# Two transformer blocks on one core: chosen rows fetched into the weights' ring and worked off in pairs from within the query projection on

## The chip, the cores and the metric

The kernel runs on one core of one Trainium2 chip. A time is the device time of one execution in microseconds (us), and what counts is the median of several runs. TensorE is called PE, VectorE DVE, ScalarE ACT, GpSimd POOL and SyncE SP, as the profile does.

## What is computed

A sequence of 256 tokens with 1024 numbers each goes through two blocks. The first has a gated mixer, a recurrent mixer and 32 experts, the second two attentions and a layer that looks up rows (`peer`). The change lies in that last layer and in the final norm behind it:

```python
def peer(xn, w_q, sub_keys, u, v):                      # xn: 256 tokens x 1024
    q = (xt @ w_q).reshape(t, PEER_HEADS, 2, PEER_HALF)  # 8 heads, two halves of 128
    sc = jnp.einsum("thpc,hpnc->thpn", q, sub_keys)      # 128 scores for each half
    top_s, top_i = lax.top_k(sc, PEER_TOPK)              # the best 16 of each half
    cand_s = top_s[:, :, 0, :, None] + top_s[:, :, 1, None, :]
    cand_i = top_i[:, :, 0, :, None] * PEER_NKEYS + top_i[:, :, 1, None, :]
    best_s, best_pos = lax.top_k(cand_s, PEER_TOPK)      # 16 of the 256 sums
    idx = jnp.take_along_axis(cand_i, best_pos, axis=-1) # 8 x 16 = 128 rows of 16384
    gate = jax.nn.softmax(best_s, axis=-1)
    ...
        act = jnp.einsum("cd,ced->ce", xc, u[ic])
        hid = jax.nn.gelu(act) * gc
        return jnp.einsum("ce,ced->cd", hid, v[ic])
x = x + peer(rmsnorm(x, norm2_g), ...); return rmsnorm(x, norm_f_g)
```

Each token picks 128 rows of a table whose rows hold 1024 numbers of u and 1024 of v, in fp32. For 256 tokens this is 32768 rows of 8 KB, 268.4 MB in all.

## The kernel before, in words

Everything is in one program whose order is written by hand (`manual_schedule`): each engine takes its instructions in the order in which the Python code emits them. Weights come over SP's queue in tiles of 16 KB per partition (4096 fp32 numbers) through a ring of `NRING` = 6 buffers, `rg[0]`; `get` and `free` move it on. A weight tile is used in eight slices; `chunk` splits a slice into a high and a low part, `sh` on ACT (line 164) and `sl` on DVE (line 165), up to two slices ahead of PE. `drive` runs a projection slice by slice and takes `per` steps of a second piece of work between slices.

The last layer handles the 256 tokens as two halves `tt` of 128, a token on each partition. After `rows_rstd` and `row_scale` come `WARM[5]` = 20 idle multiplications, the transposes of `to_T` and four query projections `projT` (line 234), each over one tile of `w_q` and two heads. `best` (lines 1204 to 1231) multiplies the queries with the keys (line 1210) and finds the best 16 of each half on DVE, for both `tt`. `choose(tt, i)` (lines 1136 to 1189) makes 32 row numbers `ei` and gates `gt` for one `tt` and two heads out of it, in 11 steps. `choose(0, 0)` rides in the third projection. The other seven are spread over the row loop, a step behind each row.

"Row k" below is one fetch of the loop `for k in range(256)`: the k-th chosen row of all 128 tokens of a half, 128 x 8 KB = 1 MB, by one indirect DMA from POOL (line 1259). `fetch` has `NR` = 13 buffers of its own, `rw`, on the right side of the memory where the ring was, and goes out `AHEAD` = 9 rows early. `first` (line 1264) multiplies the u half with the normed token `xr` on DVE and sums. `gelu` runs on ACT for four rows at a time, `second` multiplies with the gates on DVE (line 1274), makes a diagonal `dg` for each row on ACT (line 1277) and adds the v half to `acc` on PE (line 1280). `acc`, four banks of PSUM, is started with the residual by four multiplications (line 1245) just ahead of the loop. `final(0)` is emitted at row 132, `final(1)` at the end.

The lines that set the pace of the loop:

```python
for k in range(256):
    while nk < min(256, k + AHEAD):
        ...
        fetch(nk)
    first(k)
    if k % 4 == 3: gelu(k // 4)
    if k % 4 == 1 and k > 4: second(k // 4 - 1)
```

## Time and profile before

| | |
|---|---|
| median of 3 runs | 1532.22 us (1531.4 to 1534.25) |
| the profiled execution's own time | 1527.95 us |
| its span, first to last instruction | 1526.2 us |
| granted TensorE clock, mean of the span | 0.955 |
| PE / DVE / ACT / POOL busy | 86% / 52% / 26% / 27% |
| read from HBM in the span | 528.08 MB, 347 GB/s |
| of it chosen rows (POOL's queue) | 268.45 MB |

All times in rows are microseconds from the start of the span. The granted clock is a share of 2.4 GHz: 1.00 is 2.4 and 0.50 is 1.2 GHz. A PE multiplication of fp32 stands as two records in the trace, so a row of the loop has four records on PE.

### The profile page before, as it was taken

What the parts mean: (1) busy time and instruction counts of PE and PEld (TensorE: products, weight loads), DVE (VectorE), ACT (ScalarE), POOL (GpSimd) and SP (SyncE); (2) the same over time, 40 slices, a digit from 0 to 9 for tenths busy, and PEclk for the clock granted to TensorE, in tenths of its full rate; (3) what the DMA queues carried; (4) which work ended last, traced back from release to release, by engine and by line L of the source; (5) the groups of instructions that cost most, each with busy time, mean ns of one, the idle gap of its engine ahead of it and who ended that gap; (6) DMA issues with size and microseconds to landing.
All of it is one profiled execution on the core that took longest, in us unless ns stands there. A gap on an engine that the chain in (4) does not pass through costs nothing.

```text
span 1526.2 us, 16072 instructions
## 1 busy us (share of the span) xinstructions
PE 1307.3 (86%) x5543; PEld 708.8 (46%) x5543; DVE 794.6 (52%) x1852; ACT 395.1 (26%) x881; POOL 406.5 (27%) x363
## 2 busy tenths in 40 slices
PE   9899999999999898999999577878877778778776
PEld 7676344434434433978979433333332323333332
DVE  4766222222222223677677998778554545544443
ACT  6634011110111112556655232222111111111111
POOL 1211000000000002142120354444444445445441
PEclk9999999999999999999999889899999999999998
DMA  9526899999999999553220869999999999999993
GB/s 390 220 111 275 363 428 427 427 427 426 428 427 427 427 429 426 211 207 125 111 97 1 350 275 419 421 419 420 420 420 419 420 420 420 419 420 420 420 420 163
DMA packets 57747, 530.21 MB, mean 347 GB/s; under 512 B 6592, under 2 KB 6848, under 8 KB 9408
## 3 DMA queue, kind: packets, MB, share of 16 engines
q0 software_dynamic: 37936, 272.65, 43.4%
q1 hardware_dynamic: 19440, 256.35, 40.4%
q8 instruction: 46, 0.75, 0.2%
q14 instruction: 37, 0.30, 0.1%
q10 hardware_dynamic: 288, 0.16, 0.0%
HBM read 528.08 MB, written 1.05 MB: 347 GB/s over the span
## 4 chain that ended last, share of the span: by engine, by line
DMA 33%; PE 23%; issue 8%; DVE 6%; POOL 5%; ACT 1%; POOLq 0%; DVEq 0%; ACTq 0%
DMA rw<-in_uv_dram,ei 27%; PE b L234 6%; PE b L816 5%; POOL rw L1259 4%; DMA w<-in_w_gate_dram 4%; PE acc L1280 2%; PE b L854 2%; DMA w<-in_w_down_dram 2%; PE b L263 1%; DVE jk L1264 1%; PE b L247 1%; DVE sl L165 1%; PE b L763 1%; PE b L777 1%; PE b L111 1%
## 5 line engine op out<-in xcount | busy, mean ns | idle before, releaser
L1280 PE MATMUL acc<-rw,dg 128*128 128x512 f32 x1024 | 498.3, 644 | 151.6 <-ACT dg L1277 151.6
L1264 DVE SCALAR_TENSOR_TENSOR jk<-rw,xr 128x1024 f32<-128x1024 f32 x256 | 314.2, 1227 | 245.0 <-DMA rw<-in_uv_dram,ei 243.8
L1280 PEld LDWEIGHTS acc<-rw,dg 128*128 128x128 f32 x1024 | 205.2, 206 | 444.7 <-issue 230.5
L1259 POOL DMA_INDIRECT rw<-in_uv_dram,ei x256 | 306.5, 1197 | 385.6 <-PE acc L1280 283.6
L816 PE MATMUL b<-w,xg 128*64 128x512 f32 x1024 | 238.5, 605 | 10.5 <-DMA w<-in_w_gate_dram 8.2
L165 DVE TENSOR_TENSOR sl<-w,sh 128x512 fp32r<-128x512 f32 (+1 forms) x193 | 137.4, 719 | 81.4 <-ACT sh L164 80.6
L1277 ACT ACTIVATE dg<-kc,act 128x128 f32<-128x128 f32 x256 | 81.8, 390 | 284.3 <-DVE act L1274 284.3
L816 PEld LDWEIGHTS b<-w,xg 128*64 128x64 f32 x1024 | 82.5, 139 | 155.0 <-issue 134.0
L164 ACT ACTIVATE sh<-w 128x512 fp32r<-128x512 f32 (+1 forms) x200 | 120.7, 620 | 106.9 <-PE b L234 63.4
L854 PE MATMUL b<-w,hT 128*64 128x512 f32 x512 | 116.2, 595 | 6.6 <-ACT hT L125 5.5
L810 POOL TENSOR_TENSOR Dw<-Dw,Wt 128x256 f32<-128x256 f32 x16 | 9.9, 618 | 389.7 <-DVE Dw L809 389.7
L234 PE MATMUL b<-nT,sh 128*128 128x256 f32 x576 | 106.8, 286 | 3.3 <-ACT sh L164 1.7
L234 PEld LDWEIGHTS b<-nT,sh 128*128 128x128 f32 x576 | 89.0, 190 | 9.4 <-issue 4.7
L779 DVE TENSOR_TENSOR res<-res,b 128x512 f32<-128x512 f32 x64 | 40.0, 683 | 100.9 <-PE b L777 100.9
L234 PE MATMUL b<-nT,sl 128*128 128x256 f32 x288 | 81.8, 284 | 3.0 <-DVE sl L165 2.9
L859 DVE SCALAR_TENSOR_TENSOR eo<-b,gs,eo 128x512 fp32r<-128x512 f32 x32 | 24.0, 751 | 114.7 <-ACT eo L858 112.0
L854 PEld LDWEIGHTS b<-w,hT 128*64 128x64 f32 x512 | 39.0, 137 | 71.4 <-issue 61.0
L1269 ACT ACTIVATE act<-act 128x4 f32<-128x4 f32 x64 | 13.1, 205 | 227.1 <-DVE jk L1264 227.1
L823 DVE TENSOR_TENSOR hs<-hs,b 128x512 f32<-128x512 f32 x16 | 11.0, 688 | 105.9 <-PE b L816 105.9
L247 PE MATMUL b<-sh,nT 128*128 128x512 f32 (+1 forms) x192 | 58.2, 380 | 0.5 <-ACT sh L164 0.5
L234 PEld LDWEIGHTS b<-nT,sl 128*128 128x128 f32 x288 | 54.7, 190 | 4.1 <-DVE sl L165 4.1
L858 ACT ACTIVATE eo<-b,gs 128x512 fp32r<-128x512 f32 x32 | 22.0, 687 | 115.5 <-PE b L854 89.0
(407 smaller groups left out, 1323.5 us busy)
## 6 DMA issues: line engine op xcount, KB each, us to landing
w<-in_w_gate_dram SPq DMA_DIRECT2D x32, 2048.0 KB, 18.4
w<-in_w_up_dram SPq DMA_DIRECT2D x32, 2048.0 KB, 20.5
w<-in_w_down_dram SPq DMA_DIRECT2D x32, 2048.0 KB, 18.3
w<-in_w_in_dram SPq DMA_DIRECT2D x13, 2048.0 KB, 16.6
w<-in_w_out_dram SPq DMA_DIRECT2D x4, 2048.0 KB, 13.2
w<-in_w_q_dram SPq DMA_DIRECT2D x4, 2048.0 KB, 8.1
rw<-in_uv_dram,ei POOLq DMA_INDIRECT x256, 15.7
w<-in_w_in_dram SPq DMA_DIRECT2D x4, 512.0 KB, 7.3
```

The source lines that it names most:

```text
L164: nc.scalar.activation(hi, src, AF.Copy)
L165: (eng or nc.vector).tensor_tensor(lo, src, hi.bitcast(F32), op=ALU.subtract)
L234: nc.tensor.matmul(dst, l[:, c * 128:(c + 1) * 128], x[:, r, k, :], start=(k == 0 and c % 2 == 0 and i == 0), stop=(k == nk - 1 and i == 2 ...
L247: nc.tensor.matmul(bs[tt][:, :n], x[:, l, k, tt * 128:(tt + 1) * 128], r[:, :n], start=(k == 0 and i == 0), stop=(k == 7 and i == 2))
L779: nc.vector.tensor_tensor(rs, rs, b, op=ALU.add)
L816: nc.tensor.matmul(dst[64 * j:64 * j + 64, :], xg[:, k, 2 * pr + j, :], w[j][:, k * 512:(k + 1) * 512], start=(k == 0), stop=(k == 7))
L854: nc.tensor.matmul(bh[half][64 * j:64 * j + 64, :], hT[:, f, 64 * j:64 * j + 64], w[j][:, f * 1024 + half * 512:f * 1024 + half * 512 + 51 ...
L859: nc.vector.scalar_tensor_tensor(eo[:, 1, v], bh[half], wc, eo[:, 0, v].bitcast(F32), op0=ALU.mult, op1=ALU.subtract)
L1259: nc.gpsimd.indirect_dma_start(got[k], None, A["uv"], bass.IndirectOffsetOnAxis(ap=ei[tt][:, s:s + 1], axis=0))
L1264: nc.vector.scalar_tensor_tensor(junk, got[k][:, 0:D], 1.0, xr[:, tt], op0=ALU.mult, op1=ALU.mult, accum_out=act[tt][:, s:s + 1])
L1277: nc.scalar.activation(dg, ident, AF.Copy, scale=v[:, j:j + 1])
L1280: nc.tensor.matmul(acc[tt][hf], dg, rw[:, D + hf * 512:D + (hf + 1) * 512], start=False, stop=(s + j == 127), skip_group_check=True)
```

## The change

Rows no longer have buffers of their own. `fetch` takes a tile of the weights' ring, which holds two rows, and fetches a pair of rows into it. A pair goes out when its row numbers are there (`chosen`) and when the tiles of weights and of rows that are not yet freed leave one of the six buffers. The ring stays open to the end; `NR` and `AHEAD` are gone.

The choices stand in a list `todo`, those of half 0 first, each `seq(best(tt, i), choose(tt, i))` with 3 + 11 steps for one half alone. The scores `sc` of all heads get a place of their own; the keys are multiplied right behind each projection. A projection but the last takes `RQ` = 1.6 steps of `todo` per slice (`filler`), and `fetch` is tried behind each step. With the fourth projection the rows are worked off beside it: `alongside` emits a pair (`places`) and two steps of `todo` per slice, and goes on so to the end. A pair is two `first`, one `gelu` over two rows, and for each row the gate as a copy with a scale on ACT (line 1269 of the changed kernel), the diagonal and the two multiplications. The last pair is worked off row by row. The start of `acc` moves ahead of the norm. `norm_f` is loaded behind the four projections.

```diff
-        with pool("p4", 1) as p4, pool("p4b", 2) as p4b:
+        def fetch():
+            while row_st["next"] < min(256, chosen[0]) and len(src) + row_st["next"] // 2 < st["freed"] + row_st["done"] // 2 + NRING:
+                k = row_st["next"]
+                w = rg[0].tile([128, 4096], F32, tag="w", name="w")
+                for j in range(2):
+                    tt, s = divmod(k + j, 128)
+                    got[k + j] = rw = w[:, j * 2 * D:(j + 1) * 2 * D]
+                    nc.gpsimd.indirect_dma_start(rw, None, A["uv"], bass.IndirectOffsetOnAxis(ap=ei[tt][:, s:s + 1], axis=0))
+                row_st["next"] += 2
+        def step():
+            while todo and next(todo[0], StopIteration) is StopIteration:
+                todo.pop(0)
+            fetch()
+        for tt in range(2):
+            for hf in range(2):
+                nc.tensor.matmul(acc[tt][hf], ident, res[:, tt, hf * 512:(hf + 1) * 512], start=True, stop=False, skip_group_check=True)
...
-        pr_ = pk.enter_context(pool("pr", NR, side="right"))
...
+        def second(k, n):
+            tt, s = divmod(k, 128)
+            v = act[tt][:, s:s + n]
             nc.scalar.activation(v, v, AF.Gelu)
-            nc.vector.tensor_tensor(v, v, gt[tt].rearrange("p h r -> p (h r)")[:, s:s + 4], op=ALU.mult)
-            for j in range(4):
+            for j in range(n):
+                nc.scalar.activation(v[:, j:j + 1], v[:, j:j + 1], AF.Copy, scale=gf[tt][:, s + j:s + j + 1])
                 dg = pd.tile([128, 128], F32, name="dg")
                 nc.scalar.activation(dg, ident, AF.Copy, scale=v[:, j:j + 1])
...
+        def places():
+            for k in range(0, 256, 2):
+                while row_st["next"] <= k + 1:
+                    step()
+                n = 1 if k == 254 else 2
+                for j in range(0, 2, n):
+                    for i in range(j, j + n):
+                        first(k + i)
+                    second(k + j, n)
+                fetch()
+                if k == 132:
+                    final(0)
+                yield
+        def alongside():
+            for _ in pl:
+                step()
+                yield
+                step()
+        for i in range(4):
+            qT = pq2.tile([128, 4, T], F32, name="qT")
+            drive(projT(8, n4, lambda hh, b: evac(flat(qT[:, 2 * hh:2 * hh + 2, :]), b, eng="a")), al if i == 3 else fill, 1 if i == 3 else RQ)
...
+            todo.insert(i, seq(best(0, i), choose(0, i)))
+        todo += [seq(best(1, i), choose(1, i)) for i in range(4)]
...
+        for _ in al:
+            pass
```

Line numbers of the changed kernel are one or two lower than those of before for the same code. Three places show what moves.

DVE behind the query projections, before: the lines 1220 to 1230 are `best`, line 1264 is a row's multiplication, 1142 and on is `choose(0, 1)`.

```order
L1220 MAX vi_5853<-sc 128x8 x4
L1222 MATCH_REPLACE s__6720<-vi_5853,sc 128x128 x4
L1225 MAX_INDEX i_1_5855<-vi_5853,sc 128x8 x4
L1227 MAX vi_5853<-s__6720 128x8 x4
L1230 MAX_INDEX i_1_5855<-vi_5853,s__6720 128x8 x4
L1264 SCALAR_TENSOR_TENSOR jk,act_5850<-rw,xr 128x1024
L1142 TENSOR_SCALAR vi_5852<-i_0_5854 128x2x16
L1143 CAST vi_5852<-i_0_5854 128x2x16
```

DVE in the fourth projection, after: `sl` is the low part of a weight slice; the others are the same kinds of rows, with the row's multiplication now in line 1262 and the end of `choose(0, 1)` (line 1187) ahead of it.

```order
L1187 TENSOR_TENSOR gt_5848<-gt_5848,bs__6523 128x32
L164 TENSOR_TENSOR sl<-w,sh 128x512
L1262 SCALAR_TENSOR_TENSOR jk,act_5850<-w,xr 128x1024 x2
L1197 MAX vi_5852<-sc 128x8 x4
L1199 MAX_INDEX i_0_5854<-vi_5852,sc 128x8 x4
L164 TENSOR_TENSOR sl<-w,sh 128x512
L1202 MATCH_REPLACE sc<-vi_5852,sc 128x128 x4
L1204 MAX vi_5852<-sc 128x8 x4
L1262 SCALAR_TENSOR_TENSOR jk,act_5850<-w,xr 128x1024 x2
```

Rows are multiplied from the first slices of the fourth projection on, with 64 rows chosen by then, where before the first row stood behind all projections and all of `best`, with 32 rows chosen.

PE just behind the out projection (line 263), before: line 111 is the idle multiplications of `warm`, a pair of records for each.

```order
L263 MATMUL b<-sh,mg 128x512 x2
L263 MATMUL b<-sl,mg 128x512
L263 MATMUL b<-sh,mg 128x512
L111 LDWEIGHTS zero
L111 MATMUL b<-zero 128x512
```

PE in the same place, after: line 1240 starts `acc`, line 110 is the idle multiplications of `warm`.

```order
L262 MATMUL b<-sh,mg 128x512 x2
L262 MATMUL b<-sl,mg 128x512
L262 MATMUL b<-sh,mg 128x512
L1240 MATMUL acc_5863<-res,kc 128x512
L1240 MATMUL acc_5864<-res,kc 128x512
L1240 MATMUL acc_5865<-res,kc 128x512
L1240 MATMUL acc_5866<-res,kc 128x512
L110 LDWEIGHTS zero
L110 MATMUL b<-zero 128x512
```

The four starts of `acc` stood behind the last keys' multiplication before (line 1245); now they stand ahead of the idle multiplications and of the transposes behind these.

ACT at the very end, before: line 1269 is the gelu of four rows, 1277 their diagonals, 1286 is `final(1)`.

```order
L1269 ACTIVATE act_5851<-act_5851 128x4
L1277 ACTIVATE dg<-kc,act_5851 128x128 x4
L1286 ACTIVATE scr_9248,ss<-acc_5865 128x512
L1286 ACTIVATE scr_9248,ss<-acc_5866 128x512
L1472 UNCONDITIONAL_BRANCH
```

ACT at the very end, after: gelu in line 1267, gate in 1269, diagonal in 1271, `final(1)` in 1283.

```order
L1269 ACTIVATE act_5851<-act_5851,gt_5849 128x1
L1271 ACTIVATE dg<-kc,act_5851 128x128
L1267 ACTIVATE act_5851<-act_5851 128x1
L1269 ACTIVATE act_5851<-act_5851,gt_5849 128x1
L1271 ACTIVATE dg<-kc,act_5851 128x128
L1283 ACTIVATE scr_9356,ss<-acc_5865 128x512
L1283 ACTIVATE scr_9356,ss<-acc_5866 128x512
```

Behind the last row only that row's own gelu, gate and diagonal are left, where before four rows waited for it.

## Rows read from the trace of the kernel before

**Rows 1.** The page: a costly group (count, busy us, mean ns, idle before, releaser).

```profile
L1264 DVE SCALAR_TENSOR_TENSOR jk<-rw,xr 128x1024 f32<-128x1024 f32 x256 | 314.2, 1227 | 245.0 <-DMA rw<-in_uv_dram,ei 243.8
```

**Rows 2.** Chain that ended last, 900 to the end, by line.

```profile
by line: DMA rw<-in_uv_dram,ei 63.7%; issue 17.2%; POOL rw L1259 10.0%; PE acc L1280 5.6%; DVE jk L1264 1.6%; POOLq L1259 0.3%; ACT dg L1277 0.3%; DVE oh L1176 0.1%; DVE scr L1292 0.1%; DVEq L1472 0.1%; POOLq L1472 0.1%; POOL rf L1289 0.1%;
```

**Rows 3.** Busy by stretch: engines, granted clock, share of the transfer engines, GB/s.

```profile
820.00:840.00 20.00, 18.55 (x151) 17.83 (x149) 18.88 (x79) 11.61 (x19) 0.00 (x0) 1.00 0.00 1
...
880.00:884.00 4.00, 0.00 (x0) 0.00 (x0) 3.93 (x19) 1.58 (x3) 0.00 (x0) 0.50 0.03 12
884.00:888.00 4.00, 2.37 (x3) 1.17 (x4) 4.00 (x8) 2.70 (x6) 0.00 (x0) 0.50 0.00 0
...
904.00:960.00 56.00, 42.80 (x93) 17.74 (x92) 45.76 (x124) 14.41 (x36) 32.24 (x24) 0.96 1.01 420
```

**Rows 4.** Timeline of POOL (start, us, [idle before]), and issue to landing, 840 to 910.

```profile
842.80 1.07 POOL L1259 DMA_INDIRECT rw<-in_uv_dram,ei  x1 [42.80 <-issue]
...
865.82 0.94 POOL L1259 DMA_INDIRECT rw<-in_uv_dram,ei  x1 [0.30 <-issue]
889.69 1.22 POOL L1259 DMA_INDIRECT rw<-in_uv_dram,ei  x1 [22.93 <-PE acc L1280]
...
DMA to landing us min/median/max: 5.9/12.4/13.1
```

**Rows 5.** Timeline of DVE: two rows' multiplications, 160 rows apart.

```profile
1109.01 1.23 DVE L1264 SCALAR_TENSOR_TENSOR jk<-rw,xr 128x1024 f32<-128x1024 f32 x1 [1.26 <-DMA rw<-in_uv_dram,ei]
...
1508.09 1.23 DVE L1264 SCALAR_TENSOR_TENSOR jk<-rw,xr 128x1024 f32<-128x1024 f32 x1 [1.25 <-DMA rw<-in_uv_dram,ei]
```

**Rows 6.** Timeline, 1110 to 1132: two groups of four rows on PE, three fetches.

```profile
1110.86 8.83 PE L1280 MATMUL acc<-rw,dg 128*128 128x512 f32 x16 [2.84 <-ACT dg L1277]
...
1116.53 1.99 POOL L1259 DMA_INDIRECT rw<-in_uv_dram,ei  x1 [1.90 <-PE acc L1280]
1118.82 0.94 POOL L1259 DMA_INDIRECT rw<-in_uv_dram,ei  x1 [0.30 <-issue]
1120.84 7.13 PE L1280 MATMUL acc<-rw,dg 128*128 128x512 f32 x16 [1.15 <-ACT dg L1277]
```

**Rows 7.** Timeline of PE: idle multiplications and transposes; the start of `acc`.

```profile
790.05 4.48 PE L111 MATMUL b<-zero 128*128 128x512 f16 x20 [1.26 <-DVE res L606]
794.37 1.91 PE L185 MATMUL b<-kc,scr 128*128 128x128 f32 x16
...
865.45 3.60 PE L1245 MATMUL acc<-res,kc 128*128 128x512 f32 x8
```

**Rows 8.** Timeline of DVE: start of `best`, `choose(0, 0)` from end to end, one half's `best`.

```profile
813.13 0.69 DVE L165 TENSOR_TENSOR sl<-w,sh 128x512 fp32r<-128x512 f32 x1 [2.53 <-ACT sh L164]
813.74 0.87 DVE L1220 MAX8 vi<-sc 128x8 f32<-128x128 f32 x4
...
827.30 0.18 DVE L1142 TENSOR_SCALAR vi<-i 128x32 f32<-128x32 uint32 x1
...
834.15 0.69 DVE L165 TENSOR_TENSOR sl<-w,sh 128x512 fp32r<-128x512 f32 x1 [0.82 <-ACT sh L164]
...
842.29 0.87 DVE L1220 MAX8 vi<-sc 128x8 f32<-128x128 f32 x4
...
846.97 0.86 DVE L1220 MAX8 vi<-sc 128x8 f32<-128x128 f32 x4
```

**Rows 9.** Groups of ACT and DVE, 790 to the end (columns as in rows 1).

```profile
L1277 ACT ACTIVATE dg<-kc,act 128x128 f32<-128x128 f32 x256 | 81.8, 390 | 284.3 <-DVE act L1274 284.3
L1269 ACT ACTIVATE act<-act 128x4 f32<-128x4 f32 x64 | 13.1, 205 | 227.1 <-DVE jk L1264 227.1
L1269 ACT ACT_TABLE_LOAD x8 | 10.3, 1283 | 0.1
...
L1274 DVE TENSOR_TENSOR act<-act,gt 128x4 f32<-128x4 f32 x64 | 10.1, 158 | 0.3 <-ACT act L1269 0.3
```

**Rows 10.** Timeline of PE at the end of the program: the last rows.

```profile
1504.97 14.00 PE L1280 MATMUL acc<-rw,dg 128*128 128x512 f32 x32 [1.45 <-ACT dg L1277]
```

More of the change, by code (lines that the diff above doesn't have):

```diff
@@ L40 @@
 LOOK = 3
-NR = 13
-AHEAD = 9
 GLV = 0.5, 0.5
@@ L55 @@
 R4 = 2
+RQ = 1.6
 STG = 4
@@ L1233, in _body @@
-            fb = iter(())
-            for i in range(4):
-                qT = p4b.tile([128, 4, T], F32, name="qT")
-                drive(projT(8, n4, lambda hh, b: evac(flat(qT[:, 2 * hh:2 * hh + 2, :]), b, eng="a")), fb, 1)
-                run(fb)
-                fb = best(i, qT) if i != 1 else seq(choose(0, 0), best(i, qT))
-            run(fb)
-        ringctx.close()
-        c2.close()
-        for tt in range(2):
-            for hf in range(2):
-                nc.tensor.matmul(acc[tt][hf], ident, res[:, tt, hf * 512:(hf + 1) * 512], start=True, stop=False, skip_group_check=True)
@@ L1293, in final @@
                 nc.sync.dma_start(out[tt * 128:(tt + 1) * 128, v], scr[:, v])
-        todo = [(tt, i) for tt in range(2) for i in range(4)]
-        done = 1
-        fc = choose(*todo[1])
-        nk = 0
-        for k in range(256):
-            while nk < min(256, k + AHEAD):
-                while nk // 32 >= done:
-                    if next(fc, StopIteration) is StopIteration:
-                        done += 1
-                        fc = choose(*todo[done]) if done < 8 else iter(())
-                fetch(nk)
-                nk += 1
-            first(k)
-            if k % 4 == 3:
-                gelu(k // 4)
-            if k % 4 == 1 and k > 4:
-                second(k // 4 - 1)
-            if done < 8 and next(fc, StopIteration) is StopIteration:
-                done += 1
-                fc = choose(*todo[done]) if done < 8 else iter(())
-            if k == 132:
-                final(0)
@@ new lines, in _body @@
+        fill = filler()
+        pl = places()
+        al = alongside()
+        for i in range(4):
+            qT = pq2.tile([128, 4, T], F32, name="qT")
+            drive(projT(8, n4, lambda hh, b: evac(flat(qT[:, 2 * hh:2 * hh + 2, :]), b, eng="a")), al if i == 3 else fill, 1 if i == 3 else RQ)
+            for tt in range(2):
+                b = bank()
+                for j in range(4):
+                    nc.tensor.matmul(b[:, j * 128:(j + 1) * 128], qT[:, j, tt * 128:(tt + 1) * 128], ky[:, 4 * i + j, :], start=True, stop=True)
+                evac(sc[:, tt, i].rearrange("p a b -> p (a b)"), b, eng="a")
+            todo.insert(i, seq(best(0, i), choose(0, i)))
@@ L1318, in _body @@
+        todo += [seq(best(1, i), choose(1, i)) for i in range(4)]
+        fg = pj.tile([128, D], F32, name="fg2")
+        nc.sync.dma_start(fg, row(A["norm_f"], D))
+        for _ in al:
+            pass
         final(1)
+        pk.close()
+        ringctx.close()
+        c2.close()
 def mm_k(nc, dst, lhs, rhs, n):
```

76 lines of the change are left out of this document (32 added, 44 removed).

## The prediction, made before the changed kernel ran

> **What bounds the kernel now.** I read the chain of waits first. From 900 on, 63.7% of it is the transfer of chosen rows; PE has 5.6% and DVE 1.6% [rows 2]. DVE's multiplication of a row agrees: 243.8 us of the 245.0 us that DVE sat idle ahead of it were ended by a landing row [rows 1]. From 904 on the transfer engines are full (share 1.01, 420 GB/s) while DVE, PE and POOL are not [rows 3]. So the loop runs at the pace of its transfers. Two rows' multiplications 160 rows apart start at 1109.01 and 1508.09 [rows 5]: 399.08 / 160 = 2.494 us a row, 256 rows = 638.5 us. Nothing in the change alters the bytes or the shape of a fetch, so I keep the 2.494. What can move is the time at which the stream starts, how long it runs dry, and what follows the last row.
>
> All three can be read. The first fetch goes out at 842.80 [rows 4]; ahead of it the engines stand still (1 GB/s from 820 to 840) [rows 3]. The last row is multiplied at 1508.09 [rows 5], 665.3 us after the first issue. Take off 638.5 and the first row's own way (issue to landing 5.9 at least [rows 4], less 2.5), and **23.4 us of dry transfer engines** are left. Most of it has a place: thirteen fetches are out by 865.82, the fourteenth follows at 889.69 [rows 4], and from 880 to 888 the engines are empty (12 and 0 GB/s) while DVE is full, with the choice of rows 32 to 63 [rows 3]. Thirteen rows last until 842.8 + 5.9 + 12 x 2.494 = 878.6; the fourteenth can't land before 889.69 + 5.9 = 895.6, 14.5 us later than in an unbroken stream. The tail: PE works from 1504.97 for 14.00 us, to 1518.97 [rows 10], 10.9 us after the last row's multiplication began. Behind that stand 7.2 us to the end of the span, which the change leaves alone.
>
> **Start of the stream.** The four starts of `acc` took 3.60 us on PE behind all projections, where PE waited for rows anyway [rows 7]; taking them away there gives nothing. In their new place they stand ahead of the 20 idle multiplications, and the transposes follow these without a gap (790.05 + 4.48 = 794.5) [rows 7]. The row scaling is over about when the transposes start, so no cover is left and I charge 3.5 us to everything behind.
>
> The chosen rows need `choose(0, 0)`. Before, it rides in the third projection; now `best` of one half (3 steps) and `choose` (11 steps) fit the second: 9 yields x 1.6 = 14 steps. DVE sets the pace there. One half's `best` takes 846.97 - 842.29 = 4.7 us. `choose` runs from 827.30 to 842.29 with seven slices (0.65 each, by start to start) and a wait of 0.82 between: 9.6 us. Eight slices of the projection are 5.2. Together 19.5 us, from 813.74 (first `best`) + 3.5 [rows 8]: **first issue at 836.7, 6.1 us earlier.** The first pairs need two free ring tiles and the tiles of the two `w_q` used up, so four pairs go out at once and a fifth when the third projection is through; nothing of weights is in their way.
>
> **Dry time.** (a) Ten rows is all until the first pair is done. They last to 836.7 + 5.9 + 9 x 2.494 = 865.0. The first pair is emitted at the fourth projection, one more round of 19.5 us and a seam between projections of about 2.5 (the wait of DVE there [rows 8]) after the first issue: 858.7. It takes two multiplications 2.5, a table load and gelu 1.28 + 0.2, gate and diagonal about 0.6 [rows 9], and PE. A group of four rows took 7.13 us at the granted clock 1.0 that a gap of 1.15 us left, and 8.83 after a gap of 2.84 [rows 6], so a pair is 3.6 to 4.4. With 5.9 for the new fetch it lands at 873.0 instead of 867.5: 5.5 dry. (b) In the fourth projection a round does one pair, two steps of choices and one slice. DVE: 2.5 + 2 x (4.7 + 9.6) / 14 + 0.65 = 5.2, and it waits about 1 us for the slice's high part, which stands behind gelu, gates and diagonals on ACT (0.2 + 4 x 0.2 to 0.4). That is 6.2 against 4.99 for two rows; five or six such rounds until tiles are ahead again: 6.5. **12 instead of 23.4.** Ends: 5.5, if the rounds keep pace, and 23, if the opening is as poor as before.
>
> Behind it: until the choices are done a pair costs DVE 2.5 + 2.0 = 4.5 of 4.99 us, afterwards 2.5. A fetch of a pair now waits on PE for the pair six ahead, and further fetches and one small POOL operation of `final(0)` queue behind that wait. A pair is free 1.3 + 0.2 + 0.2 + 0.4 + 3.6 = 5.7 us after its second row lands. By then two more rows have landed, and eight of the twelve are still on their way, 20 us of transfers. So a late pair costs nothing until it is some 15 us late. The fetch's other wait, on the fetch eight ahead, is the same before and after.
>
> **Gates on ScalarE.** DVE loses 64 operations, 10.1 us in all, between multiplications that waited for rows anyway: no gain. ACT gets 256 small operations and 64 more gelus at 0.2 (gelu over four columns is the nearest row): 64 us, of 284.3 us of idle time ahead of the diagonals [rows 9]. On the path they stand only in the tail and in (b), where they are counted. The Trainium skill, ScalarE: Activation LUTs, Rules for kernel authors, speaks against this: it gives multiplications to VectorE. Its section What ACT_TABLE_LOAD costs prices such an operation with a pointer scale at about 0.28 us, which as an estimate from that page makes 72 us of ACT for the gates instead of 51. Either way they are covered, and the sum would change by 0.1 us in the tail.
>
> **Tail.** The last row goes alone: multiplication 1.3, gelu 0.2, gate 0.2, diagonal 0.4, handovers about 0.3, PE 1.8 at the full clock or 3.6 at the half: 4.2 to 6.0. I take 4.8, against 10.9. **6.1 earlier.**
>
> **Sum.** Last row's multiplication at 836.7 + 5.9 + 255 x 2.494 + 12 = 1490.6, end of PE at 1495.4 instead of 1518.97: 23.6 us less (6.1 start, 11.4 dry time, 6.1 tail). The span would be 1502.6. The profiled execution (1527.95, span 1526.2) lies 4.3 below the median of the runs shown, so I take the difference and not the span: 1532.2 - 23.6 = **1508.6**.
>
> **Rivals.** *The opening stays as poor as before.* An issue takes POOL 0.94 alone and 1.99 beside a row's multiplication on DVE [rows 6]. A pair's two issues now stand in a row, where the engines wait for them. One more us in each, over eight dry rounds, with DVE's delays in (b) doubled, keeps the dry time at 23: 1532.2 - 12 = 1520. Against it: later pairs are issued ahead of need. The Trainium skill, GPSIMD Engine Reference, Specifications, says why such an issue would stretch: GpSimd shares its SBUF interfaces with VectorE, and instructions with two SBUF inputs contend. The two durations agree with it. Chance 0.14.
>
> *The rounds keep pace,* with only the first gap left: 1502. For it: DVE's 5.2 is hardly over 4.99, and the wait for the slice is my guess. Chance 0.10.
>
> *No earlier start:* the choices hang on something that I don't see, the first issue comes at 842.8 + 3.5 and the dry time stays, so that only the tail is won: 1532.2 + 3.5 - 6.1 = 1529.6, the same within what a measurement here can tell (0.2%, 3 us). Chance 0.03.
>
> *Slower:* PE's clock. PE now gets a pair, 3.6 us of work, and then waits 1.4, all the time. Where PE had been idle the granted clock stood at 0.50 [rows 3]; after a gap of 2.84 a group took 1.7 longer, after 1.15 it didn't [rows 6]. If the new rhythm kept the clock down, a pair would take up to 7.1, more than the 4.99 of its transfer, and PE would be the bound. It decides from 4.99 + 23.6 / 128 = 5.17 us a pair, a mean granted clock of 0.69 in the loop. At 0.6 a pair is 5.95: 128 x 0.96 = 123 us more, 1631. Against it: a PE that is late has no gaps, and a gapless PE ran at 1.0. Chance 0.04.
>
> **How the numbers follow.** Forecast 0.69, rivals 0.14, 0.10, 0.03, 0.04. The range takes in the two ends of the dry time, 1502 and 1520, and 1 us of the tail at the low end: 1501 to 1520. Faster by over 0.2% is 0.69 + 0.14 + 0.10 = 0.93, same 0.03, slower 0.04.
>
> **What would show it.** The first fetch at 836 to 838; the idle multiplications 3.5 us later; a gap of 5 us in the transfers near 865 and small ones to about 900; 420 GB/s and 2.494 us a row from then on; pairs on PE of about 3.6 us at a granted clock near 1; the last row's multiplication near 1491 and PE's end 4 to 6 us behind it. It is wrong if transfers run dry in the later loop, if a row takes other than 2.494, or if the first pair is not worked off near 859.

## The result and the profile after

The changed kernel takes 1511.44 us, the median of 4 runs (1508.44 to 1511.71), against 1531.83 for the kernel before in the same comparison: a ratio of 0.9864, 95% interval 0.985 to 0.9877, or 20.4 us less. (In the later comparisons the kernel before took 1531.2 to 1531.9.) The forecast was 1508.6 with a range of 1501 to 1520, and faster by over 0.2% with a chance of 0.93. So sign, range and rough size hold. One of the three large terms does not, by half.

The profiled execution took 1511.64 us, its span 1509.6. Up to the out projection ahead of the last layer both kernels run the same instructions, yet its last multiplication on PE starts at 788.40 in the trace of before and at 791.17 in that of after; over all the profiled executions below it lies between 788.4 and 793.1. So I count from that multiplication ("the anchor") where two traces are compared. Timelines of PE, start and duration, before and then after:

```profile
788.40 0.39 PE L263 MATMUL b<-sh,mg 128*128 128x512 f32 x1
```

```profile
791.17 0.39 PE L262 MATMUL b<-sh,mg 128*128 128x512 f32 x1
792.84 3.70 PE L1240 MATMUL acc<-res,kc 128*128 128x512 f32 x8 [1.28 <-DVE res L605]
796.38 4.48 PE L110 MATMUL b<-zero 128*128 128x512 f16 x20
```

The idle multiplications start 5.21 behind the anchor instead of 1.65 [rows 7]: 3.56 later, for the four starts of `acc` that now stand ahead of them.

Costly groups of the page of after, the answer to [rows 1], and three groups of ACT, 790 to the end, the answer to [rows 9] (count | busy us, mean ns | idle before, releaser):

```profile
L1274 PE MATMUL acc<-w,dg 128*128 128x512 f32 x1024 | 477.4, 612 | 157.3 <-ACT dg L1271 157.1
L1224 POOL DMA_INDIRECT w<-in_uv_dram,ei x256 | 365.0, 1426 | 308.2 <-DMA w<-in_uv_dram,ei 143.4
L1262 DVE SCALAR_TENSOR_TENSOR jk<-w,xr 128x1024 f32<-128x1024 f32 x256 | 313.0, 1223 | 212.8 <-DMA w<-in_uv_dram,ei 211.2
```

```profile
L1271 ACT ACTIVATE dg<-kc,act 128x128 f32<-128x128 f32 x256 | 102.7, 401 | 8.4
L1269 ACT ACTIVATE act<-act,gt 128x1 f32<-128x1 f32 x256 | 73.4, 287 | 4.2
L1267 ACT ACTIVATE act<-act 128x2 f32<-128x2 f32 x129 | 26.2, 203 | 410.4 <-DVE jk L1262 410.4
```

DVE still waits for rows, and ACT, with 73 us of gates more, still has 410 us in which it waits for DVE: the loop is still bound by its transfers. The busy time by stretch of after, beside [rows 3] (length, busy us of PE, PEld, DVE, ACT and POOL, granted clock, share of the transfer engines, GB/s):

```profile
838.00:864.00 26.00, 15.05 (x101) 12.89 (x101) 24.41 (x101) 9.67 (x19) 11.11 (x10) 0.95 0.92 374
864.00:872.00 8.00, 8.00 (x23) 4.04 (x23) 6.62 (x29) 2.12 (x6) 1.87 (x2) 0.74 0.37 126
872.00:896.00 24.00, 20.36 (x81) 12.04 (x80) 19.03 (x52) 10.29 (x26) 12.91 (x10) 1.00 0.96 357
896.00:924.00 28.00, 22.87 (x78) 12.45 (x77) 20.00 (x68) 9.57 (x29) 8.18 (x9) 0.88 1.01 422
924.00:928.00 4.00, 4.00 (x11) 1.85 (x10) 3.93 (x18) 1.49 (x5) 2.09 (x3) 1.00 0.72 238
928.00:1480.00 552.00, 414.49 (x897) 162.55 (x897) 337.94 (x753) 181.53 (x579) 329.47 (x225) 0.99 1.01 421
1480.00:1490.00 10.00, 6.81 (x16) 2.52 (x14) 4.55 (x8) 2.10 (x8) 0.00 (x0) 1.00 1.01 419
1490.00:1494.00 4.00, 3.67 (x8) 1.44 (x8) 2.23 (x3) 0.87 (x3) 0.00 (x0) 1.00 0.31 127
1494.00:1498.00 4.00, 2.75 (x8) 1.28 (x8) 1.51 (x5) 2.39 (x8) 0.00 (x0) 1.00 0.05 23
```

With 421 GB/s as full, a stretch of length L that moves G GB/s was dry for L x (1 - G / 421). That makes 5.6 us from 864 to 872 (the first dry stretch), 3.6 from 872 to 896 (the rounds of the fourth projection) and 1.7 from 924 to 928: 10.9 us. Behind that the transfers are full to 1490. The last two lines are the end of the stream, 2.8 + 3.8 = 6.6 us short of full; they hold up no row, since the last rows are still multiplied 2.48 us apart, the last at 1497.96.

The fetches on POOL (timeline, [idle before <- who ended it]) show the two places, and PE and DVE what stood ahead of them:

```profile
838.36 1.07 POOL L1224 DMA_INDIRECT w<-in_uv_dram,ei  x1 [33.03 <-DVE bs__6300 L1186]
...
869.35 0.94 POOL L1224 DMA_INDIRECT w<-in_uv_dram,ei  x1 [14.98 <-PE acc L1274]
...
924.40 0.95 POOL L1224 DMA_INDIRECT w<-in_uv_dram,ei  x1 [10.71 <-PE acc L1274]
```

```profile
862.67 6.40 PE L1274 MATMUL acc<-w,dg 128*128 128x512 f32 x8 [6.28 <-ACT dg L1271]
...
911.07 1.95 PE L1323 MATMUL b<-ky,qT 128*128 128x128 f32 x16
918.15 16.27 PE L1274 MATMUL acc<-w,dg 128*128 128x512 f32 x32 [5.13 <-ACT dg L1271]
```

```profile
859.07 1.22 DVE L1262 SCALAR_TENSOR_TENSOR jk<-w,xr 128x1024 f32<-128x1024 f32 x1
...
912.79 0.87 DVE L1197 MAX8 vi<-sc 128x8 f32<-128x128 f32 x4 [7.65 <-ACT sc L124]
...
1497.96 1.23 DVE L1262 SCALAR_TENSOR_TENSOR jk<-w,xr 128x1024 f32<-128x1024 f32 x1 [1.24 <-DMA w<-in_uv_dram,ei]
```

The first pair took PE 6.40 us instead of the 3.70 of the loop, after 6.28 us in which PE stood idle; the eleventh fetch had to wait for it. The second place: DVE comes to `best(0, 3)` and waits 7.65 us for its scores, whose multiplication with the keys (line 1323, at 911.07) stands on PE behind queued pairs; PE then idles 5.13 and takes 16.27 for the next four pairs, 14.8 at the pace of the loop.

From the anchor to the end of the span it is 737.8 us before (1526.2 - 788.40) and 718.4 after, 19.4 less. The three terms:

| | before | after | change | forecast |
|---|---|---|---|---|
| anchor to first fetch | 54.4 | 47.2 | -7.2 | -6.1 |
| first fetch to the last row's multiplication | 665.3 | 659.6 | **-5.7** | **-11.4** |
| that multiplication to the end of the span | 18.1 | 11.6 | -6.5 | -6.1 |

### The profile page after: what moved, and what is told of

Same layout as the page of the kernel before. It is cut to its first block, busy times and chain, and to the rows that moved or that the text cites. A ratio compares the mean times of both kernels' runs of the same rounds, so it can differ in the third digit from the quotient of the medians.

```text
span 1509.6 us, 16190 instructions
## 1 busy us (share of the span) xinstructions
PE 1287.5 (85%) x5543; PEld 697.2 (46%) x5543; DVE 787.4 (52%) x1788; ACT 487.0 (32%) x1200; POOL 464.9 (31%) x363
## 4 chain that ended last, share of the span: by engine, by line
DMA 37%; PE 22%; DVE 9%; issue 4%; ACT 2%; POOL 1%; POOLq 0%; DVEq 0%; ACTq 0%
DMA w<-in_uv_dram,ei 31%; PE b L815 6%; DMA w<-in_w_gate_dram 6%; PE b L233 6%; DVE jk L1262 3%; PE b L853 2%; PE acc L1274 1%; PE b L262 1%; DVE sl L164 1%; PE b L246 1%; PE b L762 1%; PE b L776 1%; PE b L110 1%; POOL w L1224 1%; ACT sh L163 1%
## 5 line engine op out<-in xcount | busy, mean ns | idle before, releaser
L1274 PE MATMUL acc<-w,dg 128*128 128x512 f32 x1024 | 477.4, 612 | 157.3 <-ACT dg L1271 157.1
L1224 POOL DMA_INDIRECT w<-in_uv_dram,ei x256 | 365.0, 1426 | 308.2 <-DMA w<-in_uv_dram,ei 143.4
L1262 DVE SCALAR_TENSOR_TENSOR jk<-w,xr 128x1024 f32<-128x1024 f32 x256 | 313.0, 1223 | 212.8 <-DMA w<-in_uv_dram,ei 211.2
L1274 PEld LDWEIGHTS acc<-w,dg 128*128 128x128 f32 x1024 | 187.9, 192 | 440.9 <-ACT dg L1271 248.9
L1267 ACT ACTIVATE act<-act 128x2 f32<-128x2 f32 x129 | 26.2, 203 | 410.4 <-DVE jk L1262 410.4
L1271 ACT ACTIVATE dg<-kc,act 128x128 f32<-128x128 f32 x256 | 102.7, 401 | 8.4
L1269 ACT ACTIVATE act<-act,gt 128x1 f32<-128x1 f32 x256 | 73.4, 287 | 4.2
## 6 DMA issues: line engine op xcount, KB each, us to landing
w<-in_w_down_dram SPq DMA_DIRECT2D x32, 2048.0 KB, 19.4
w<-in_w_out_dram SPq DMA_DIRECT2D x4, 2048.0 KB, 13.4
```

Source lines behind the costliest of these rows:

```text
L1224: nc.gpsimd.indirect_dma_start(rw, None, A["uv"], bass.IndirectOffsetOnAxis(ap=ei[tt][:, s:s + 1], axis=0))
L1262: nc.vector.scalar_tensor_tensor(junk, got[k][:, 0:D], 1.0, xr[:, tt], op0=ALU.mult, op1=ALU.mult, accum_out=act[tt][:, s:s + 1])
L1269: nc.scalar.activation(v[:, j:j + 1], v[:, j:j + 1], AF.Copy, scale=gf[tt][:, s + j:s + j + 1])
L1271: nc.scalar.activation(dg, ident, AF.Copy, scale=v[:, j:j + 1])
L1274: nc.tensor.matmul(acc[tt][hf], dg, rw[:, D + hf * 512:D + (hf + 1) * 512], start=False, stop=(s + j == 127), skip_group_check=True)
```

## The experiments

All but two are edits of the kernel after; E7 and E7b edit the kernel before. "First fetch", "first row" and "last row" (the start of that row's multiplication on DVE) count from the anchor of each trace, "end" is the time from the last row's multiplication to the end of the span. The three dry columns are worked out from the GB/s of each run's stretches by the formula above (421.5 as full): from 25 to 36 us behind the run's first fetch, from 36 to 60, and from 60 to 95.

| run | median us | ratio to before, 95% | first fetch | first row | last row | end | dry 25-36 | 36-60 | 60-95 |
|---|---|---|---|---|---|---|---|---|---|
| before | 1531.8 | | 54.4 | 86.3 | 719.7 | 18.1 | 0.1 | 13.3 | 0.1 |
| after | 1511.4 | 0.985 - 0.9877 | 47.2 | 67.9 | 706.8 | 11.6 | 5.8 | 3.6 | 1.8 |
| E1 acc later | 1512.2 | 0.9863 - 0.9893 | 46.2 | 66.9 | 706.8 | 11.7 | 4.6 | 3.7 | 3.4 |
| E2 RQ 1.0 | 1507.8 | 0.9831 - 0.9856 | 53.3 | 61.9 | 704.9 | 13.4 | 0.1 | 0.0 | 0.1 |
| E3 one step | 1510.4 | 0.9841 - 0.9871 | 47.2 | 67.9 | 704.0 | 13.4 | 6.1 | 1.7 | 0.0 |
| E4 gates on DVE | 1510.7 | 0.9851 - 0.988 | 47.2 | 67.9 | 704.8 | 11.6 | 5.1 | 2.9 | 1.2 |
| E5 pairs held back | 1519.7 | 0.9909 - 0.9936 | 47.2 | 86.3 | 716.3 | 11.6 | 8.0 | 10.0 | 1.1 |
| E6 last pair whole | 1514.2 | 0.9878 - 0.9907 | 47.2 | 67.9 | 707.9 | 13.2 | 5.3 | 3.2 | 3.0 |
| E7 before, last 4 rows single | 1531.3 | 0.9985 - 1.0005 | 54.4 | 86.6 | 720.4 | 16.7 | 0.1 | 13.6 | 0.2 |
| E7b before, last 8 rows single | 1525.2 | 0.9944 - 0.9973 | 54.4 | 86.4 | 720.2 | 11.9 | 0.1 | 13.7 | 0.0 |
| E9 acc at first pair | 1510.6 | 0.9854 - 0.9884 | 44.4 | 65.5 | 704.3 | 11.7 | 4.3 | 4.7 | 2.4 |
| E10 E9 and RQ 1.0 | 1506.2 | 0.9823 - 0.985 | 50.4 | 60.7 | 701.1 | 11.7 | 0.0 | 0.1 | 0.6 |
| E11 E9, RQ mixed, one step | 1507.9 | 0.9831 - 0.9862 | 44.4 | 67.4 | 700.9 | 13.4 | 5.7 | 2.1 | 0.0 |
| E12 pairs from third projection | 1504.9 | 0.9811 - 0.9842 | 44.4 | 50.6 | 700.0 | 11.4 | 0.1 | 0.0 | 6.4 |

### The tail alone (E7, E7b, E6)

E7 and E7b put this into the loop of before. The cut shows E7b; E7 has `k >= 252` and leaves out the last two lines. In both `second(63)` behind the loop goes; in E7b `second` in its old place ends ahead of row 248:

```python
+            if k >= 248:
+                one(k)      # gelu, gate on DVE, dg, two multiplications, for this row
             elif k % 4 == 3:
                 gelu(k // 4)
...
+            if k == 247:
+                second(61)
```

> The kernel before, with its last four rows worked row by row (gelu, gate on VectorE, diagonal, PE for each) instead of as one group. It measures the tail alone. Theory: PE ends 4.8 us behind the start of the last multiplication instead of 10.9, so 6.1 less than the kernel before: 1525.7. Rival: PE stays at the half clock that its last group had (14.00 us for four rows, 3.5 a row against 2.49 that a row takes to come), is late from the first of the four rows on and ends about 1515.6 in that trace's time instead of 1518.97: 3.4 less, 1528.4.

> The kernel before with its last eight rows worked row by row and the group ahead of them sent to PE as soon as its gates are due (with only four, that group was queued behind rows 252 and 253 and PE ended 9.5 us behind the start of the last multiplication). Theory: at the full clock a row takes PE 1.85 and comes every 2.49, so PE is through with the earlier ones and ends 4.5 us behind the last multiplication instead of 10.9: 6 us less than before, 1525.2. Rival: the clock falls to the half with so many short gaps, a row takes 3.6, PE is late by all eight rows, and the time is that of before or longer, 1531.

E7 won nothing, 1531.3, and for neither reason that I had given. My second one rested on a misreading: the 14.00 us of [rows 10] are `x32`, eight rows at the full clock, not four at the half. PE at the end of E7 and of E7b:

```profile
1506.71 1.98 PE L1291 MATMUL acc<-rw,dg 128*128 128x512 f32 x4 [0.71 <-ACT dg L1288]
1509.19 1.98 PE L1291 MATMUL acc<-rw,dg 128*128 128x512 f32 x4 [0.50 <-ACT dg L1288]
1511.01 7.03 PE L1280 MATMUL acc<-rw,dg 128*128 128x512 f32 x16
1517.88 3.60 PE L1291 MATMUL acc<-rw,dg 128*128 128x512 f32 x8
```

```profile
1502.16 13.90 PE L1291 MATMUL acc<-rw,dg 128*128 128x512 f32 x32
```

In E7 the group ahead of the single rows (line 1280, 7.03 us) was emitted behind two of them, so it kept PE busy when the last row came (1511.96): PE's end was 9.5 us behind that. E7b sends the group first, and PE ends at 1516.06, 4.7 behind the last multiplication (1511.38). It takes 1525.2, 6.4 less than the kernel before in the same comparison (1531.6), as its theory had it. So a tail of single rows is worth 6 us by itself, as long as nothing older is queued ahead of it.

E6 takes the split of the last pair out of after (`n = 2` for every k):

> The kernel after with its last pair worked as a pair instead of row by row. Theory: behind the start of the last multiplication stand 1.3 + 0.2 for gelu + 0.7 for gate and diagonal + 3.7 of PE and the handovers, 6.2 us instead of the 4.5 read in after: 1.7 more, 1513.1. Rival: PE is still busy with the pair ahead when the last row comes, so that splitting wins nothing: 1511.4 with 4.5 to 5 us in the trace.

```profile
1499.75 3.70 PE L1274 MATMUL acc<-w,dg 128*128 128x512 f32 x8 [1.08 <-ACT dg L1271]
```

That is E6's last pair on PE: its end is 6.0 us behind the last multiplication (1497.46), against 4.5 in after (1495.29 + 7.13 - 1497.96, below). 1.5 for the split, near the 1.7 expected. The medians differ by 2.8; by the traces 1.1 of it lies ahead of the last row, which this edit doesn't touch.

### Where the starts of acc stand (E1, E9)

E1 moves the four starts behind the keys of the first projection, E9 right ahead of the first pair:

```python
-        for tt in range(2):
-            for hf in range(2):
-                nc.tensor.matmul(acc[tt][hf], ident, res[...], start=True, ...)
...
         def places():
             for k in range(0, 256, 2):
...
+                if k == 0:            # E9; E1: in the projection loop, if i == 0
+                    ...the four multiplications
```

> The kernel after, with the four starts of acc put behind the keys' multiplications of the first projection, where PE waits for DVE anyway. My theory: in their new place nothing covers them, since idle multiplications, transposes and projections follow one another on PE; so all that follows comes 3.5 us earlier and the time is 1508, against 1511.4 of the kernel after; the transposes start 3.5 us earlier counted from the last multiplication of the out projection. Rival: the row scaling on ACT and DVE (over at 797.3 in the trace of after, while the idle multiplications last until 800.9) or the first splitting of the weights would then end last, and only a part or nothing is won: 1510 to 1511.4.

> The kernel after with the four starts of acc right ahead of the first pair, where PE stood idle for 6.3 us and then took 6.40 instead of 3.70 for that pair at the half clock. (Behind the first projection, the place of e1, they held the second projection's first slice: DVE waited 1.74 us for it.) Theory: everything up to the first pair comes 3.5 us earlier, counted from the last multiplication of the out projection, and the filled gap brings the first pair back to 4 us, so the first dry stretch falls from 5.8 to about 3; what that wins is given back near 924, where the stream waits for the choice of rows 96 to 127 behind the last scores: 3.5 us less than after, 1508. Rival: as in e1, the start is given back as well, 1511.4. Third: nothing is given back, 1505.

In E1 the transposes came 3.5 us earlier (5.99 behind the anchor instead of 9.53), but the time stayed, as the rival had it. The start went in two pieces. The starts now stood ahead of the second projection's first slice, and DVE waited 1.74 us for that slice: the first fetch was only 1.0 earlier (0.8 us has no place). That 1.0 was given back: the first dry stretch fell by 1.2, the third grew by 1.6, and the last row came at 706.8 as in after. PE in E9:

```profile
853.22 3.59 PE L1298 MATMUL acc<-res,kc 128*128 128x512 f32 x8
859.68 3.70 PE L1271 MATMUL acc<-w,dg 128*128 128x512 f32 x8 [2.87 <-ACT dg L1268]
```

The first fetch is 2.8 earlier, and the first pair takes 3.70 at the full clock, since PE now idles 2.87 ahead of it and not 6.28. Yet the dry stretches sum to 11.4, as in after (11.2): the first fell by 1.5, the other two grew by 1.7. The last row is 2.5 earlier in the trace; the medians, 0.8 apart, can't tell that from nothing. Of my 3.5 us on the path, 3.5 arrive at the transposes and 2.8 at the first fetch; whether all of it reaches the end, this run doesn't show.

### Pairs within the fourth projection (E5)

```python
-            drive(projT(...), al if i == 3 else fill, 1 if i == 3 else RQ)
+            drive(projT(...), fill, RQ)
```

> The kernel after, but the fourth projection carries choices alone, as the second and third do, and the pairs start behind it. Theory: the ten rows fetched ahead run out at the same time, the first pair is done some 17 us later (869 to 886), so the first dry stretch grows from 6 to about 22 us; in exchange there are no long rounds (about 7 us dry in after) and no wait for the last scores (2.5): 7 us more, 1518. Rival: pairs beside the projection are worth nothing, since what they win they give back in long rounds and a low clock: 1511 or less.

1519.7, and the last row 9.5 later than in after: the ten rows run out at the same time and the first pair's PE work starts at 879.90 (89.9 behind the anchor) instead of 862.67 (71.5). Dry to 60 us behind the first fetch: 18 us instead of 9.4. So this part of the change is worth 8 us, near the 7 of the theory.

### What makes the rounds long (E3, E4)

E3 takes one of the two steps out of `alongside`; E4 puts `nc.vector.tensor_tensor(v, v, gf[tt][:, s:s + n], op=ALU.mult)` in the place of the gates on ACT.

> The kernel after, with one step of the choices per pair instead of two (in the fourth projection and behind it). It asks what makes the rounds of the fourth projection 6.1 to 7.2 us long where two rows' transfer takes 4.99. Theory A, DVE's load: a round loses about 1 us of choices, rounds fall to 5.2 and the dry stretches between 870 and 896 nearly go: 5 to 6 us less, 1506. Theory B, the wait for the slice's high part behind gelu, gates and diagonals on ACT: DVE then waits longer instead, rounds stay above 6, and the time is within 1.5 of 1511.4. Whichever holds, the choices of rows 64 on come later and so the wait of DVE for the last scores near 905 and the dry stretch at 924 should shrink, at most 2.5 us of it.

> The kernel after with the gates on VectorE again, one multiplication per pair behind gelu. Theory: covered either way. ACT loses 73 us, DVE gets 20; in the rounds of the fourth projection the slice's high part comes 0.5 us sooner while DVE waits 0.3 for gelu: within 1.5 us of 1511.4, and the mean of ACT's share falls without an effect. Rival (the rule that gives such multiplications to VectorE): the 256 gates on ACT cost time in rounds and tail, 3 us or more: 1508 or less. Second rival: DVE, in order, now stands behind gelu for each pair and the loop gets longer: 1514 or more.

DVE, first multiplications of two rounds and the wait between, in after and then in E3:

```profile
872.41 1.22 DVE L1262 SCALAR_TENSOR_TENSOR jk<-w,xr 128x1024 f32<-128x1024 f32 x1
...
877.06 0.69 DVE L164 TENSOR_TENSOR sl<-w,sh 128x512 fp32r<-128x512 f32 x1 [1.85 <-ACT sh L163]
...
878.51 1.21 DVE L1262 SCALAR_TENSOR_TENSOR jk<-w,xr 128x1024 f32<-128x1024 f32 x1
```

```profile
879.24 1.22 DVE L1262 SCALAR_TENSOR_TENSOR jk<-w,xr 128x1024 f32<-128x1024 f32 x1
...
883.90 0.69 DVE L164 TENSOR_TENSOR sl<-w,sh 128x512 fp32r<-128x512 f32 x1 [1.45 <-ACT sh L163]
884.51 1.22 DVE L1262 SCALAR_TENSOR_TENSOR jk<-w,xr 128x1024 f32<-128x1024 f32 x1
```

6.1 us and 5.3 us a round. The wait for the slice's high part is in both; one step less makes the round shorter by 0.8. It halves the dry time of the rounds (3.6 to 1.7) and takes the third stretch away; the last row comes 2.8 earlier. Of that, 1.8 is lost behind the last row (the column "end"; why is shown at E2), and the medians, 1.0 apart, can't tell the rest from nothing. By the rounds theory A came closer, by the time theory B; neither holds whole. In E4 DVE waits 0.27 for gelu in each pair and 0.2 to 1.0 for the slice instead of 1.3 to 1.9: rounds of 5.5 to 5.7, 0.5 less, and 2.0 in the last row, nothing that the medians could show. 0.7 of the 2.0 lies in the first stretch and goes with PE's clock there (the first pair took 5.22 and not 6.40), not with the gates. Gates on ACT cost a little where DVE waits for ACT and nothing in the loop.

### Start against first pair (E2, E10, E11, E12)

E2 sets `RQ = 1.0`. E10 is E9 with it. E11 is E9 with 1.6 in the second projection, 1.0 in the third and one step in `alongside`. E12 is E9 with the pairs from the third projection on:

```python
-            drive(projT(...), al if i == 3 else fill, 1 if i == 3 else RQ)
+            drive(projT(...), al if i >= 2 else fill, 1 if i >= 2 else RQ)
...
-            for _ in pl:
+            for c, _ in enumerate(pl):
                 step()
                 yield
-                step()
+                if c < 11 and c % 2:
+                    step()
```

> The kernel after with RQ = 1.0 instead of 1.6, one step of the choices per slice in the second and third projection. Theory: an early stream only empties its ten rows sooner. The first fetch comes 8 to 9 us later (rows 0 to 31 are chosen five slices into the third projection), but the first pair comes as early as before, so the first dry stretch (5.8 us) goes, and with it most of the 3.6 in the rounds and the 1.9 near 924, since the choices and the last scores are waited for later: about 2 us less than after, 1509.6. Rival: the long rounds of the fourth projection, not the ten rows, empty the transfers; then 8 us of start are lost for 5.8 of the first stretch and the rounds stay: 1514 or more.

> The same with RQ = 1.0. In e2 the transfers never ran dry behind their start, so a start that is 3.5 us earlier has nothing to give back to. Theory: 3.5 us less than e2, 1504.3, first fetch 3.5 earlier counted from the out projection, no dry stretch. Rival: a dry stretch opens again near 870 or 912, since the choices are no earlier in use than before, and 2 us or more are lost: 1506.5 or more.

> The starts of acc ahead of the first pair, 1.6 steps a slice in the second projection only, 1.0 in the third, one step per pair from the fourth on. Theory: the first fetch is as early as in e9 (7 us ahead of e2's kind), the third projection is 4 us shorter so that the first pair comes in time (first dry stretch under 1 us), the rounds lose 2 us as in e3, nothing near 924: 8 to 11 us less than after, 1501 to 1503. Rival: ten rows last 25 us from the first fetch on, and with the first fetch this early the stretch stays at 3 us or more; then it is no better than e10, 1504 to 1506.

> The starts of acc ahead of the first pair, RQ = 1.6 in the second projection, and the pairs from the third projection on (in after: from the fourth), with three steps of the choices per two pairs for the first eleven pairs and one per pair from there. It asks whether the early stream was lost only for want of a pair to work off. Theory: the first fetch comes 44.4 us behind the start of the last multiplication of the out projection, as in e9; eight rows are out at once (two of the ring's tiles still hold weights) and last until 67.7; the first pair starts at about 53 instead of 68, is through at 60, and the ninth row lands at 66: no first dry stretch. Rounds of 5.3 against 4.99 cost 2 to 3 us over eighteen rounds. The last row's multiplication comes at 697 instead of 701 (e10): 1502, 4 us less than e10. Rival: with four to five tiles left for rows, eighteen rounds instead of nine each run dry by 1 us and eat more than the start won: 1510 or more.

E2 gives away 6.1 us of start, and its last row comes 1.9 earlier than in after. Against what I had expected, the first pair came earlier too, by 6.0 us (the column "first row"), since the second and third projections carry fewer choices. Its stretches:

```profile
842.00:852.00 10.00, 7.23 (x56) 6.46 (x54) 9.90 (x47) 5.45 (x8) 7.58 (x8) 1.00 0.75 268
852.00:940.00 88.00, 75.29 (x236) 39.13 (x236) 78.51 (x246) 38.73 (x106) 44.38 (x37) 0.96 1.01 422
```

Full from the first rows on, through all of the fourth projection. The rounds there are 6.2 us long as well (multiplications of first rows at 850.89, 857.05 and 863.23), so long rounds alone don't dry the transfers; they do so when the ten rows are used up as they begin. In this execution the end took 13.4 us instead of 11.6, so that from the anchor to the end of the span it is no faster than after (718.3 and 718.4); the medians are 3.7 apart, with intervals that overlap. PE's last four rows in E2 and in E10:

```profile
1491.22 8.83 PE L1274 MATMUL acc<-w,dg 128*128 128x512 f32 x16 [2.24 <-ACT dg L1271]
```

```profile
1488.84 7.13 PE L1271 MATMUL acc<-w,dg 128*128 128x512 f32 x16 [2.24 <-ACT dg L1268]
```

After the same 2.24 us of idleness the clock stood at 0.52 from 1494 to 1496 in E2 and at 1.00 in E10. E3 and E11 had the 8.83 too. So 1.7 us of the end are a matter of PE's clock and not of the edits. E10 adds the earlier start, now kept: first fetch 2.9 earlier than E2, last row 3.8. It takes 1506.2, between its theory (1504.3) and its rival (1506.5 or more); 1.6 us by the medians is no proof alone. E11 fetches 6 us before E10 and its last row comes with E10's (700.9 and 701.1): its first pair was multiplied 67.4 behind the anchor, as in after (67.9) and 6.7 later than in E10, and the six us stand in the table as dry time (7.8 against 0.7). Here the rival held; I had expected the third projection to be shorter. E12 brings the first pair forward, to 842.00 (50.6 behind the anchor), and there is no first stretch at all. It loses 6.4 later, most of it where the fourth projection begins:

```profile
908.00:912.00 4.00, 3.73 (x18) 2.37 (x16) 3.96 (x16) 1.04 (x4) 1.20 (x2) 0.94 0.10 43
```

DVE waits 6.15 us ahead of that, until 900.67, for the first slice's high part, and the next pair is late. ACT shows why, and it is the wait of after near 912 in another place: the scores (line 124) wait on ACT for the keys (line 1325), which stand on PE behind queued pairs (7.03 us from 890.67), and the high part (line 163) stands behind the scores:

```profile
898.63 0.60 ACT L124 ACTIVATE sc<-b 128x512 f32<-128x512 f32 x1 [4.43 <-PE b L1325]
899.52 0.60 ACT L124 ACTIVATE sc<-b 128x512 f32<-128x512 f32 x1 [0.30 <-PE b L1325]
900.02 0.62 ACT L163 ACTIVATE sh<-w 128x512 fp32r<-128x512 f32 x1
```

Keys emitted ahead of the last pair of a projection would be the next thing to try; it wasn't tried. At 1504.9 us E12 has the lowest median of all, between its theory (1502) and its rival (1510); its interval (0.9811 to 0.9842) lies below that of after (0.985 to 0.9877), but overlaps those of E10 and E11. Last rows of 701.1, 700.9 and 700.0 say that the three are about equal by their traces.

## Why the prediction was right, and where it was not

**Start: right, 1 us too small.** The starts of `acc` cost 3.56 (3.5). The first fetch, predicted at 836.7, came at 838.36, and that execution was 2.8 late from the anchor on: 7.2 us earlier than before, against 6.1.

**Dry time: the gaps were right, the saving was not.** I put 12 us of gaps in the place of "23.4 us of dry transfer engines". The gaps came out at 10.9: 5.6 (5.5), 3.6 (6.5) and 1.7 near 924, which I had not seen. But the 23.4 was not a sum of gaps. It was all that was left between two events at 2.494 us a row, and I wrote that "most of it has a place" when 14.5 had. Three stretches of before, with two rows of the same view:

```profile
878.00:895.00 17.00, 9.37 (x17) 4.15 (x18) 16.90 (x45) 5.76 (x13) 3.23 (x3) 0.64 0.30 105
895.00:908.00 13.00, 13.00 (x32) 5.53 (x31) 12.73 (x51) 3.20 (x8) 10.31 (x8) 1.00 1.00 406
908.00:1490.00 582.00, 451.27 (x927) 185.41 (x926) 342.62 (x728) 102.72 (x310) 277.88 (x233) 0.92 1.01 420
...
1500.00:1504.00 4.00, 3.52 (x9) 1.26 (x7) 2.12 (x3) 0.00 (x0) 0.00 (x0) 1.00 0.36 147
1504.00:1508.00 4.00, 3.03 (x7) 1.44 (x8) 1.66 (x5) 1.28 (x4) 0.00 (x0) 1.00 0.05 23
```

By the same formula before has 12.8 + 0.5 = 13.3 us of gaps. Gaps against gaps, the saving was 2.4. What made 23.4 of them is a miscount: the two multiplications of [rows 5] are not 160 rows apart. Multiplications of rows by DVE, in before from 1109.01 to 1508.09 and in after from 1097.70 to 1497.96, first and last included (count: ns min/median/max, first and last start):

```profile
L1264 DVE SCALAR_TENSOR_TENSOR jk<-rw,xr x159: 1216/1225/1300, 1109.0 to 1508.1; 128x1024 f32<-128x1024 f32 x159
```

```profile
L1262 DVE SCALAR_TENSOR_TENSOR jk<-w,xr x160: 1215/1225/1227, 1097.7 to 1498.0; 128x1024 f32<-128x1024 f32 x160
```

159 multiplications are 158 rows apart: 399.08 / 158 = 2.526 us a row, 646.6 and not 638.5 for 256. So 665.3 - 646.6 - 3.4 = 15.3 us were left in before, of which 14.5 had a place, and not 23.4. The 2.494 is the distance of most neighbours; about one row in 40 comes 3.45 behind the one ahead. So the mis-sized term is the pace, and through it the dry time of before. With 2.526 the prediction's own sum gives the last row at 836.7 + 5.9 + 255 x 2.526 + 12 = 1498.7 (it came at 1497.96) and a saving of 6.1 + 3.3 + 6.1 = 15.5 us, 1516.7.

The pace changed as well, and I had held it constant: 400.26 / 159 = 2.517 in after, 2.1 us less over 256 rows. That a row "takes other than 2.494" was one of my signs of being wrong, and it came true before the change and after it. So the 5.7 of the table are 2.4 of gaps, 2.1 of pace and 1.2 that I leave open. E2 and E10 agree: with no gap to speak of, 651.6 and 650.7 from first fetch to last row leave 3.8 and 2.9 at 2.517 a row, where 2.494 leaves 9.7 and 8.8. Why the pace differs between the two kernels was not tested.

**Inside the gaps.** The first pair was priced at 3.6 to 4.4 on PE and took 6.40: I had PE's clock in the rivals and not here, though PE stood idle while DVE worked through choices and the first rows. E9 shows it, 3.70 with the gap filled. The 6.40 itself is one execution's: with the same idle time ahead (6.16 to 6.29 us) the first pair took 5.22 in E4, 5.79 in E6 and 6.70 in E3, and the first dry stretch goes with it (5.1, 5.3 and 6.1; 5.8 in after). That this stretch came out as forecast is in part luck: the first pair began 20.7 us behind the first fetch, and I had put 22.0. The rounds were 6.1 to 6.2 us long as predicted, but cost 3.6 and not 6.5. The wait for the last scores was missing: I read each queue by itself and not that `best(0, 3)` is the next step on DVE while its keys stand on PE behind queued pairs.

**Gates: right.** 287 ns each where I took 0.2 from the gelu row, 73 us in all, hidden. The Trainium skill, ScalarE: Activation LUTs, What ACT_TABLE_LOAD costs, has 0.28 us for such an operation, and the trace agrees. The advice of its section Rules for kernel authors, to leave multiplications to VectorE, made no measurable difference in E4.

**Tail: right.** PE in after:

```profile
1495.29 7.13 PE L1274 MATMUL acc<-w,dg 128*128 128x512 f32 x16 [1.25 <-ACT dg L1271]
```

4.5 us from the last row's multiplication to PE's end (4.8 predicted, 4.2 to 6.0 as the range), 7.2 from there to the end of the span as before. Of the ten runs with such a tail seven show 4.3 to 4.5 and three (E2, E3, E11) 6.2, so the low value is in part luck. E7b measured the same term by itself, 6.4 for the 6.1.

**Rivals.** The slower one fell: the clock granted in the loop was 0.99 (928 to 1480), with pairs of 3.70 and gaps of 1.25, where it was 0.92 before. No earlier start fell with the first fetch, and rounds that keep pace fell with rounds of 6.1 us against 4.99. The poor opening was half true: fetches of up to 1.9 us and long rounds were there, but the gaps stayed at 10.9. The Trainium skill, GPSIMD Engine Reference, Specifications, speaks of such contention with VectorE, and the trace of after agrees in part: all 92 issues of 1.7 us or more between 840 and 1490 overlap a row's multiplication on DVE, and the nine that overlap no work of DVE took 0.93 to 0.94. But 13 that overlap one for over 0.5 us took less than 1 us, so "0.94 alone and 1.99 beside a row's multiplication" was too simple: the 0.94 at 1118.82 [rows 6] stands beside one as well. No run here shows that long issues cost time.

That the forecast was only 2.8 us off is partly luck: 5.7 too much for dry time, less 1.1 and 0.4 too little for start and tail, about 1 us by which the medians differ by more than the traces, and 0.4 between the two medians of before. With the rows counted right, the same sum would have missed by 5 us on the other side.

## What to carry to other kernels

Count the rows between two events before you divide: 160 in the place of 158 made 8 us of dry time out of nothing. A remainder between two events is not idle time that a change can win: add up the gaps that the rows show, and where the two sums don't agree (14.5 against 23.4 here), look for the error first. When a stream goes through a ring, an earlier first fetch is worth nothing once the rows in hand run out ahead of the first release (E11 against E10; E2, whose fetch is later and whose first pair is earlier), so price the first piece of work, with the clock that PE has after its idle time. When work is cut into finer pieces for the tail, look at what was emitted ahead of it (E7).
